# Gates of two more token tiles ahead of the scan phase, and another order of the visits

## The chip, the core and the metric

The kernel runs on one core of a Trainium2 chip. The metric is the time of one execution on the device in microseconds. The median of the runs shown is 2695.26 us (2690.73 to 2696.66 us).

## The reference

The program is one layer of a backbone over 128 context tokens and 2048 latent tokens, 17 tiles of 128 tokens, with a model width of 1024. It computes in this order:

- h = modulated RMSNorm of x, and proj = h @ w_in, cut into q, k, v (3 x 512), a gate (512), 16 columns of scan coefficients, u (512) and vg (512);
- q, k, v through a convolution of width 3 and silu, q and k normalized; then a gated DeltaNet with 4 heads, forward and backward over the tokens, in chunks;
- o_a = rmsnorm(o) * silu(gate) and, per chunk of 128 tokens, o_b = gelu(u) * (ws @ layernorm(gelu(vg)) + bs);
- x = x + ga1 * (concat(o_a, o_b) @ w_out), then a second modulated norm and a squared-ReLU MLP of width 4096, and a final norm.

The recurrence that orders the scan is this step; a chunk needs the state S of the chunk before it:

```
def step(S, xs):
    qd, kd, u_c, w_c, qk_c, gl = xs
    v_new = u_c - einsum('bhck,bhkv->bhcv', w_c, S)
    o = einsum('bhck,bhkv->bhcv', qd, S) + einsum('bhcs,bhsv->bhcv', qk_c, v_new)
    S = S * exp(gl)[..., None, None] + einsum('bhck,bhcv->bhkv', kd, v_new)
```

The outputs are y for the context, y for the latent tokens, and the final states of the context.

## The kernel before, in words

The kernel has three stages. The first projects q, k and v for blocks of three token tiles and stores the normalized rows h to DRAM as a high and a low part (hH_d, hL_d). A product with full precision takes three matmuls: high by high, high by low, low by high (function mm3, lines 217 to 219). In its tail the first stage also loads and splits weights for the next stage, all eight blocks of the gate weights and seven of the eight blocks of the v weights (NV = 7), and the rows of the first HT = 4 token tiles (first_rows).

The second stage is the scan phase, and the change is in it. It has 34 units, one for each token tile and direction: first forward over tiles 0 to 16, then backward. A unit has

- prep_loads (lines 942, 964, 966): a row of decays, the tile's k-by-k products KK and its q-by-k products QK;
- 17 preparation steps: E and its two masked forms (lines 984 to 989), KK scaled and cast to AH, with X (lines 997 to 1004), Y as the transpose of X (lines 1010 and 1012), five levels of two steps each that double a triangular inverse (lines 1028 to 1051), and four closing steps;
- scan_loads, and four scan steps, which carry the state from one unit to the next (lines 959 and 1100 to 1143).

Between these, TensorE gets filler work: for each of the 17 token tiles three groups, g (gate), v and u, of eight steps of three matmuls each (group, one step for each of the eight blocks of 128 input columns). The rows of a tile come by f2_loads (line 1182) into a pool of eight buffers, and a tile needs four. After a group come its finishing steps: for g a tanh, a product and a store (lines 1197 to 1199); for v a gelu (lines 1166 to 1173) and the statistics and centring of 128 tokens (lines 1205 to 1213); for u a gelu and the spatial product (line 1220), which reads the centred vg of its tile, and a store of the result (lines 1224 and 1227). The working buffers of these steps (tags gw, vg and ug) have one buffer each. The groups share four PSUM banks, two of them named pm and two pj, with the spatial products and, later, the output projection. The first four gates use rows and buffers of the pool wp instead.

The order of the work is written out as events with a time. A unit i prepares from i - 2.46 to i - 0.03 and scans from i - 0.51 to i + 1.06 in the forward pass. All filler steps form one list, flat. Its first NF steps are put ahead of everything, at -12 or -8; the rest is spread evenly from -1.61 to 18.16 as fills, and a fill's matmuls are held behind the first matmul of the last preparation or scan step that is emitted before them. The events are emitted in order of time, and a scheduler that simulates the engines then fixes each engine's queue: what is emitted earlier has precedence among what it takes to be ready. On the chip each queue runs in that order. All DMAs are issued by SyncE's queue (SP).

At the start of the phase stand, in order of event time: gates 0 to 3 (-12), the loads of unit 0 (-10), rows of tile 0 (-9), the last block of v weights (-9), the blocks of u weights (-8.5), and then (-8) rows of tile 1, v of tile 0 and one step of u of tile 0. The third stage is the MLP; the change does not touch it.

Of the kernel before, what the change touches and what calls it, by code (L numbers as in the profile page):

```python
# [19 lines left out]
KT = D // P  # L20
DFF = 4096
NT = 17
# [23 lines left out]
NE = 4  # L46
LAG2 = 0
LAG3 = 3
NF = 46
PL = 0  # L50
HT = 4
NV = 7
# [9 lines left out]
def hybrid_step(  # L62
# [137 lines left out]
    def load_w2(gi, k):  # L200
        off = {"g": 1536, "v": 2576, "u": 2064}[gi]
        W2[gi].append(load_split(w_in[0, k * P : (k + 1) * P, off : off + 512]))
# [64 lines left out]
    with ExitStack() as ph:  # L267
# [479 lines left out]
        for bi in range(len(BLOCKS)):  # L747
# [6 lines left out]
            at = {e: n for n, e in enumerate(order)}  # L754
            tile_of = {}
            for n, (gi, h) in enumerate(order):
                u = us[n] if bi == 0 and n < 3 else feature_tile(blk, bi, gi, h)
# [154 lines left out]
    with ExitStack() as ph:  # L912
# [341 lines left out]
        def o_loads(u):  # L1254
            t = u["t"]
            u["of"], u["ga"] = w512("of"), w512("ga")
            load(out=u["of"], in_=of_d[t * P : (t + 1) * P, :])
            load(out=u["ga"], in_=gate_d[t * P : (t + 1) * P, :])
# [74 lines left out]
        def at(time, fn, kind=None):  # L1333
            events.append((time, len(events), fn, kind))

        def spread(t0, t1, steps, kind):
            for j, st in enumerate(steps):
                at(t0 + (t1 - t0) * (j + 0.5) / len(steps), st, kind)

        def scan_step(i, f):  # L1340
            def g():
                u = units[i]
                if "s" not in u:
                    u["s"] = None if i in (0, NT) else units[i - 1]["sn"] if i not in (1, NT + 1) else u["s0"]
                f()
            return g

        def after(i):

            d = 0 if i == 0 else 1  # L1350
            store(out=new_state[0, 0, d].rearrange("h k v -> k h v"), in_=units[i]["sn"])
            s0 = q32("S", 2)
            load(out=s0, in_=state_delta[0, 0, d].rearrange("h k v -> k h v"))
            units[i + 1]["s0"] = s0

        p2, p3 = WINDOWS[:8], WINDOWS[8:]
        for i, u in enumerate(units):
            w = p2 if i <= NT else p3
            at(i - 3 if i > PL else -10, u["prep_loads"])
            at(i - 1, u["scan_loads"])  # L1360
            n = len(u["prep"])
            for j, st in enumerate(u["prep"]):
                at(i - w[0] + (j + 0.5) * (w[0] - w[1]) / n, st, "prep")
            spread(i + w[2], i + w[3], [scan_step(i, f) for f in u["scan"]], "chain")
            if i in (0, NT):
                at(i + w[2] + (w[3] - w[2]) * 0.7, lambda i=i: after(i))
            if i >= NT:
                at(i, lambda u=u: o_loads(u))
                first, second = o_steps(u)
                spread(i + p3[4], i + p3[5], first, "fill")  # L1370
                spread(i + p3[6], i + p3[7], second, "fill")
                if u["t"] > 8:
                    st = h2_steps(u["t"], pj, fraw, w512, fpart, fhalf, lambda u=u: u["x2"])
                    spread(i + p3[8], i + p3[9] + 0.2, st[:5], "fill")
                    spread(i + p3[9] + 0.2, i + p3[9] + 2.1, st[5:], None)
        f2 = [f2_steps(t) for t in range(NT)]
        flat = []
        for n, (t, gi) in enumerate([(t, "g") for t in range(HT)] + [(t, gi) for t in range(HT) for gi in "vu"]
                                    + [(t, gi) for t in range(HT, NT - 2) for gi in "gvu"]
                                    + [(NT - 2, "g"), (NT - 1, "g")]  # L1380
                                    + [(t, gi) for t in (NT - 2, NT - 1) for gi in "vu"]):
            main, later = f2[t][1][gi]
            if gi == "v" and t + 1 < NT - 1 or gi == "g" and t == NT - 2:
                flat.append((KT * n - 0.5, f2[t + 1][0]))
            flat += [(KT * n + j, st) for j, st in enumerate(main)]
            flat += [(KT * n + KT + j + (0.5 if n >= HT else -0.5), st) for j, st in enumerate(later)]
        flat = [st for _, st in sorted(flat, key=lambda e: e[0])]
        at(-9, f2[0][0])
        for j, st in enumerate(flat[:NF]):
            at(-8 if j >= HT * (KT + 1) else -12, st)  # L1390
        for gi in "vu":
            for k in range(NV if gi == "v" else 0, KT):
                at(-9 if gi == "v" else -8.5, lambda gi=gi, k=k: load_w2(gi, k))
        flat = flat[NF:]
        spread(p2[4], p2[5], flat, "fill")
# [412 lines left out]
    for p, (o, n, b) in enumerate(seq):  # L1808
        u = units[n]
# [118 lines left out]
```

## Time and profile before

| | |
|---|---|
| median of the runs | 2695.26 us |
| profiled execution, its own time | 2696.7 us |
| its span, first to last instruction | 2695.0 us |
| TensorE busy | 2628.5 us (98%) |
| VectorE busy | 1866.8 us (69%) |
| ScalarE busy | 1245.5 us (46%) |
| DMA, mean over the span | 216 GB/s |
| granted TensorE clock, mean | 0.993 |

PE is TensorE's matmuls and PEld its weight loads, which overlap them; DVE is VectorE, ACT ScalarE, POOL GpSimd, SP the queue that issues DMAs. In a row of instructions in order of time stand start, duration, engine, line, operation and tiles, and in brackets the idle time before it with what ended that. In a row of a stretch stand the busy times of PE, PEld, DVE, ACT and POOL, the granted clock, the DMA share and the rate. Matmul ends are modelled, and successive matmuls overlap in the rows: their rate is read from their starts.

### The profile page before, as it was taken

What the parts mean: (1) busy time and instruction counts of PE and PEld (TensorE: products, weight loads), DVE (VectorE), ACT (ScalarE), POOL (GpSimd) and SP (SyncE); (2) the same over time, 40 slices, a digit from 0 to 9 for tenths busy, and PEclk for the clock granted to TensorE, in tenths of its full rate; (3) what the DMA queues carried; (4) which work ended last, traced back from release to release, by engine and by line L of the source; (5) the groups of instructions that cost most, each with busy time, mean ns of one, the idle gap of its engine ahead of it and who ended that gap; (6) DMA issues with size and microseconds to landing.
All of it is one profiled execution on the core that took longest, in us unless ns stands there. A gap on an engine that the chain in (4) does not pass through costs nothing.

```text
span 2695.0 us, 45202 instructions
## 1 busy us (share of the span) xinstructions
PE 2628.5 (98%) x15698; PEld 2192.3 (81%) x15698; DVE 1866.8 (69%) x3909; ACT 1245.5 (46%) x3092; POOL 229.5 (9%) x448
## 2 busy tenths in 40 slices
PE   8999999999999899999999999999999999999998
PEld 5999997788887787778887788888888787888887
DVE  5867656877777878885688775665565547774874
ACT  4655555555555656763355543332342432342441
POOL 3111203111111111110000000000000000000000
PEclk9999999999999999999999999999999999999999
DMA  8867539555555657885877797433459979876772
GB/s 297 279 202 224 183 113 299 177 157 161 160 162 157 204 191 232 269 279 181 285 221 228 212 313 228 122 104 106 121 170 371 329 265 309 272 243 215 235 252 94
DMA packets 569388, 580.91 MB, mean 216 GB/s; under 512 B 35693, under 2 KB 401693, under 8 KB 565575
## 3 DMA queue, kind: packets, MB, share of 16 engines
q1 hardware_dynamic: 569158, 578.03, 67.2%
q8 instruction: 123, 2.02, 0.3%
q14 instruction: 107, 0.87, 0.1%
HBM read 398.14 MB, written 179.74 MB: 214 GB/s over the span
## 4 chain that ended last, share of the span: by engine, by line
PE 86%; DVE 6%; DMA 5%; issue 1%; ACT 1%; POOL 0%; SPq 0%; DVEq 0%; POOLq 0%; ACTq 0%
PE f L219 17%; PE f L217 17%; PE f L218 17%; PE pj L217 6%; PE pj L219 6%; PE pj L218 6%; PE pd L959 3%; PE pm L217 1%; PE pm L219 1%; PE pm L218 1%; PE pm L321 1%; PE pt L575 1%; PE pd L1136 1%; PE pd L1137 1%; DMA qT<-qT_d 1%
## 5 line engine op out<-in xcount | busy, mean ns | idle before, releaser
L217 PE MATMUL f<-hop,zH 128*128 128x512 f32 x960 | 376.5, 393 | 1.2 <-ACT zH L1444 1.2
L218 PE MATMUL f<-hop,zH 128*128 128x512 f32 x960 | 377.1, 393 | 0.0
L219 PE MATMUL f<-hop,zL 128*128 128x512 f32 x960 | 376.9, 393 | 0.0
L217 PE MATMUL f<-hop,wH 128*128 128x512 f32 x896 | 354.0, 397 | 0.0
L219 PE MATMUL f<-hop,wL 128*128 128x512 f32 x896 | 351.3, 392 | 0.0
L218 PE MATMUL f<-hop,wH 128*128 128x512 f32 x896 | 351.1, 392 | 0.0
L1444 ACT CAST zH<-zraw 128x512 fp32r<-128x512 f32 x240 | 146.6, 620 | 287.2 <-DVE zraw L1438 86.4
L217 PEld LDWEIGHTS f<-hop,zH 128*128 128x128 f32 x960 | 180.3, 188 | 43.7 <-ACT zH L1444 1.6
L219 PEld LDWEIGHTS f<-hop,zL 128*128 128x128 f32 x960 | 180.3, 188 | 41.9 <-issue 0.9
L218 PEld LDWEIGHTS f<-hop,zH 128*128 128x128 f32 x960 | 180.2, 188 | 41.8 <-issue 0.9
L1438 DVE TENSOR_TENSOR zL<-zraw,zH 128x512 fp32r<-128x512 f32 x240 | 162.9, 686 | 69.1 <-ACT zH L1444 57.7
L219 PEld LDWEIGHTS f<-hop,wL 128*128 128x128 f32 x896 | 168.5, 188 | 37.7
L218 PEld LDWEIGHTS f<-hop,wH 128*128 128x128 f32 x896 | 168.8, 188 | 35.2
L217 PEld LDWEIGHTS f<-hop,wH 128*128 128x128 f32 x896 | 168.8, 188 | 34.7
L217 PE MATMUL pj<-kH,wH 128*128 128x386 f32 (+2 forms) x568 | 190.5, 338 | 0.3 <-DVE kH L473 0.3
L219 PE MATMUL pj<-kH,wL 128*128 128x386 f32 (+2 forms) x568 | 190.3, 335 | 0.0
L218 PE MATMUL pj<-kL,wH 128*128 128x386 f32 (+2 forms) x568 | 189.5, 334 | 0.0
L176 POOL TENSOR_TENSOR r<-rsq,nhalf 128x1 f32<-128x1 f32 (+1 forms) x38 | 23.0, 606 | 1499.3 <-DVE rsq L175 1499.3
L1438 DVE TENSOR_TENSOR wL<-raw,wH 128x512 fp32r<-128x512 f32 x112 | 76.0, 687 | 76.0 <-ACT wH L1444 74.9
L523 DVE SCALAR_TENSOR_TENSOR cv<-pj,vec,cv 128x384 f32<-128x384 f32 (+2 forms) x164 | 87.1, 539 | 58.7 <-ACT cv L520 57.4
L217 PEld LDWEIGHTS pj<-kH,wH 128*128 128x128 f32 x568 | 107.2, 189 | 4.6 <-issue 4.2
L217 PE MATMUL pj<-wH,hH 128*128 128x512 f32 x248 | 109.8, 443 | 0.0
(398 smaller groups left out, 6088.3 us busy)
## 6 DMA issues: line engine op xcount, KB each, us to landing
zraw<-z_d SPq DMA_DIRECT2D x212, 256.0 KB
raw<-in_w_ff_dram SPq DMA_DIRECT2D x128, 256.0 KB
hop<-hop_d SPq DMA_DIRECT2D x28, 1024.0 KB
z_d<-c SPq DMA_DIRECT2D x96, 256.0 KB
zraw<-s_d SPq DMA_DIRECT2D x96, 256.0 KB
raw<-in_w_mod_dram SPq DMA_DIRECT2D x80, 256.0 KB
r<-in_w_ff_dram SPq DMA_DIRECT2D x80, 256.0 KB
s_d<-s SPq DMA_DIRECT2D x64, 256.0 KB
```

The source lines that it names most:

```text
L176: G.tensor_tensor(out=out, in0=t[:np_, :n], in1=nhalf[:np_, :n], op=ALU.pow)
L217: T.matmul(ps, lh, rh, start=first and i == 0, stop=False, skip_group_check=more)
L218: T.matmul(ps, lh, rl, start=False, stop=False, skip_group_check=more)
L219: T.matmul(ps, ll, rh, start=False, stop=last and i == n - 1, skip_group_check=more)
L321: T.matmul(pm[0:2, :], scond[:, k, :], raws[k], start=k == 0, stop=k == KT - 1)
L523: V.scalar_tensor_tensor(out=cv[:, o : o + m], in0=ps[:, s + sh : s + sh + m], scalar=convw[:, w, j : j + 1], in1=cv[:, o : o + m], op0=AL ...
L575: T.matmul(ps[:, i * P : (i + 1) * P], kTt[:, i * P : (i + 1) * P], rhs[:, i * P : (i + 1) * P], start=True, stop=True)
L959: T.matmul(p[:, h, :], lhs[:, h, :], rhs[:, h, :], start=True, stop=True)
L1136: T.matmul(p[:, h, :], u["qT"][:, h, :], s[:, h, :], start=True, stop=False)
L1137: T.matmul(p[:, h, :], u["QK"][:, h, :], u["vn"][:, h, :], start=s is None, stop=True)
L1438: V.tensor_tensor(out=out, in0=a, in1=b, op=op)
L1444: A.copy(h, src)
```

## The change

The front of the filler list becomes longer and its order changes. NF goes from 46 to 62. The list now holds the gates of tiles 0 to 3, then g of tiles 4 and 5, v of 4 and 5, u of 4 and 5, then tiles 6 to 14 with g, v and u each, then v and u of tiles 0 to 3, and tiles 15 and 16 as before. The 62 steps ahead are the four gates (36 steps with their finishing steps) at -12, and g of tile 4, g of tile 5 (each with its finishing step) and v of tile 4 at -8. Rows are loaded for tile 4 at -11.5 and for tile 5 at -9.5; the rows of tile 6 are loaded ahead of u of tile 5, and from then on a tile's rows are loaded ahead of v of the tile visited before it. The loads of unit 0 move from -10 to -12.5, so they are emitted before the first gates.

No computation is added or removed.

```diff
-NF = 46
+NF = 62
...
-            at(i - 3 if i > PL else -10, u["prep_loads"])
+            at(i - 3 if i > PL else -12.5, u["prep_loads"])
...
-        for n, (t, gi) in enumerate([(t, "g") for t in range(HT)] + [(t, gi) for t in range(HT) for gi in "vu"]
-                                    + [(t, gi) for t in range(HT, NT - 2) for gi in "gvu"]
+        visits = [4, 5] + list(range(6, NT - 2)) + list(range(HT)) + [NT - 2, NT - 1]
+        after_visit = dict(zip(visits, visits[1:]))
+        for n, (t, gi) in enumerate([(t, "g") for t in range(HT)] + [(t, gi) for gi in "gvu" for t in (4, 5)]
+                                    + [(t, gi) for t in range(6, NT - 2) for gi in "gvu"]
+                                    + [(t, gi) for t in range(HT) for gi in "vu"]
                                     + [(NT - 2, "g"), (NT - 1, "g")]
                                     + [(t, gi) for t in (NT - 2, NT - 1) for gi in "vu"]):
             main, later = f2[t][1][gi]
-            if gi == "v" and t + 1 < NT - 1 or gi == "g" and t == NT - 2:
-                flat.append((KT * n - 0.5, f2[t + 1][0]))
+            if gi == "v" and t not in (4, 5, NT - 2, NT - 1) or (t, gi) in ((5, "u"), (NT - 2, "g")):
+                flat.append((KT * n - 0.5, f2[after_visit[t]][0]))
...
-        at(-9, f2[0][0])
+        at(-11.5, f2[4][0])
+        at(-9.5, f2[5][0])
         for j, st in enumerate(flat[:NF]):
             at(-8 if j >= HT * (KT + 1) else -12, st)
```

## The prediction, made before the changed kernel had run

> **What bounds the kernel now.** I read the page's engine totals first, then busy time by stretches around the start of the scan phase, then the instructions of that place in order of time on each engine, then the chain of waits. All times are of the profiled execution, which took 2696.7 us (span 2695.0 us and 1.7 us around it); the median of the runs, 2695.26 us, is 1.4 us below it.
>
> ```profile
> span 2695.0 us, 45202 instructions
> PE 2628.5 (98%) x15698; PEld 2192.3 (81%) x15698; DVE 1866.8 (69%) x3909; ACT 1245.5 (46%) x3092; POOL 229.5 (9%) x448
> ```
>
> TensorE is idle for 66 us in all. The next rows (busy time of each engine in a stretch, granted clock, DMA share, GB/s) show where some of that lies.
>
> ```profile
> 440.00:460.00 20.00, 20.00 (x92) 16.51 (x91) 5.98 (x20) 6.86 (x18) 4.19 (x4) 1.00 0.97 290
> 460.00:480.00 20.00, 11.29 (x64) 6.66 (x63) 17.40 (x43) 14.54 (x39) 8.97 (x8) 0.66 0.90 308
> 480.00:500.00 20.00, 18.55 (x148) 13.90 (x147) 17.07 (x44) 8.95 (x23) 2.56 (x3) 1.00 0.67 194
> 515.00:561.00 46.00, 44.32 (x382) 36.47 (x382) 33.35 (x95) 24.76 (x67) 5.62 (x8) 1.00 0.57 167
> 600.00:800.00 200.00, 198.40 (x1687) 164.22 (x1686) 146.10 (x424) 108.89 (x292) 24.13 (x32) 1.00 0.52 159
> ```
>
> So there is a hole at 460 to 480 us: 8.7 us idle, and a granted clock of 0.66. From 515 us the forward scan keeps TensorE full. The hole by instruction:
>
> ```profile
> 455.73 0.39 PE L217 MATMUL pm<-wH,hH 128*128 128x512 f32 x1
> 455.95 0.39 PE L218 MATMUL pm<-wL,hH 128*128 128x512 f32 x1
> 456.18 0.39 PE L219 MATMUL pm<-wH,hL 128*128 128x512 f32 x1
> 456.41 0.39 PE L217 MATMUL pm<-wH,hH 128*128 128x512 f32 x1
> ...
> 462.32 0.40 PE L1010 MATMUL pd<-ident,X 128*128 128x128 f16 x4 [0.59 <-DVE X L1004]
> ...
> 466.70 0.63 PE L219 MATMUL pm<-wH,hL 128*128 128x512 f32 x1
> 470.11 0.37 PE L1032 MATMUL pd<-Y,As 128*128 128x64 f16 x4 [2.77 <-ACT Y L1012]
> ...
> 472.54 0.37 PE L1032 MATMUL pd<-Y,As 128*128 128x64 f16 x4 [0.96 <-ACT Y L1048]
> 472.73 0.77 PE L217 MATMUL pm<-wH,hH 128*128 128x512 f32 x1
> ```
>
> Up to 466.7 us run the 41 front steps (three matmuls each; starts 0.227 us apart at full clock, so a step is 0.68 us). The first fill runs at 472.73 us, behind the sixth preparation step of unit 0 (L1032 of level 4): fills are ordered behind preparation, and the first fill's time -1.61 lies behind six of unit 0's seventeen steps from -2.46 on. What held those steps:
>
> ```profile
> 457.88 1.28 ACT L984 ACTIVATE E<-gb,gcol 128x128 f32<-128x128 f32 x4 [6.79 <-DMA gb<-g_d]
> 459.07 0.60 ACT L1002 CAST AH<-KK 128x512 f16<-128x512 f32 x1
> ...
> 467.79 0.62 ACT L1002 CAST AH<-KK 128x512 f16<-128x512 f32 x1 [3.81 <-POOL KK L999]
> ...
> 469.49 0.56 ACT L1012 CAST Y<-pd 128x512 f16<-128x512 f32 x1
> 463.98 3.77 POOL L999 TENSOR_SCALAR_AFFINE_SELECT KK<-KK 128x512 f32<-128x512 f32 x1 [1.99 <-DMA QK<-qk_d]
> ```
>
> Unit 0's copy Y (L1012) is ready to run from 462.7 us but stands in ScalarE's queue behind unit 1's AH, which waits for a GpSimd select of 3.77 us, itself behind unit 1's loads. That latency is not TensorE work, so it can be covered.
>
> **The change part by part.** *The front (46 to 62 steps of the list).* Before: 4 gate groups, v of tile 0 and one step of u 0, 41 matmul steps. After: the same 4 gates, then g 4, g 5 and v 4: 56. So 15 steps, 45 matmuls, 45 x 0.227 = 10.2 us of TensorE, leave the fills (367 steps become 352) and stand ahead of them.
>
> What that saves later depends on what sets the forward scan's pace. One unit there, from one chain row to the same of the next unit, and its matmuls:
>
> ```profile
> 627.40 1.09 PE pd L959 x8
> 650.13 1.09 PE pd L959 x8
> L217 PE MATMUL pj<-wH,hH 128*128 128x512 f32 x11 | 4.8, 433 | 0.0
> L217 PE MATMUL pm<-wH,hH 128*128 128x512 f32 x8 | 3.7, 459 | 0.0
> L1137 PE MATMUL pd<-vn,QK 128*128 128x128 f32 x8 | 1.5, 275 | 0.0
> L1032 PE MATMUL pd<-Y,As 128*128 128x64 f16 x20 | 1.4, 194 | 0.0
> 508.36 0.89 PE pj L1220 x8
> 485.35 0.28 PE L1045 MATMUL pd<-P,X 128*128 128x64 f16 x4 [0.72 <-DVE P L1036]
> 485.47 0.28 PE L1047 MATMUL pd<-X,P 128*128 128x64 f16 x4
> ```
>
> The period is 22.73 us. By starts and not by overlapping durations: 19 steps x 0.68 = 12.9 us; six groups of eight fp32 128x128 (five like L1137, one L1220) x 0.89 = 5.3 us; three lines of 20 small fp16 (like L1032), each four 0.12 us apart, 1.8 us; some 30 other fp16 matmuls, estimated from the same 0.03 us up to 0.06 us each, 1 to 2 us. That is 21 to 22 of 22.73 us: TensorE sets the pace, and the 10.2 us come off it nearly whole. I take -10.2.
>
> The Trainium skill, "Perfetto Trace Analysis", Identifying the Most-Contended Engine, says that matmul busy time doesn't tell how full TensorE is and that the weight loads' share does. That share is 164.22 of 200 us here, 82%; by it alone a fifth of the period would be free, and the saving could be nothing, as in the third rival.
>
> What it costs in front: v began at 455.73 us without a wait; from there now run 24 steps, 72 x 0.227 = 16.3 us, to 472.1 us. The nearest to a bound below: if unit 0's steps get their turns among them, the first fill comes at about 472.5 us, as now: cost 0. Above: if Y's four matmuls (L1010, earlier 462.32) come only behind the front, what stood from the copy Y to the first fill, 472.73 - 469.49 = 3.2 us, and 0.4 us for Y's matmuls follow 472.1: first fill at 475.7 us, cost 3.0. The front is earlier in emission than the preparation and its inputs are ready, so I take +3.0.
>
> *What feeds the front.* Gates need gate weights only, all built; v 0's last step and u 0 waited for theirs (first row below). The rows of tile 4 take the place of tile 0's, those of tile 5 that of tile 1's:
>
> ```profile
> 461.24 0.49 PE L217 MATMUL pm<-wH,hH 128*128 128x512 f32 x1 [0.59 <-ACT wH L191]
> ...
> 444.24 0.38 SPq L1182 DMA_DIRECT2D hH<-hH_d  x1
> ...
> 449.85 0.90 SPq L1199 DMA_DIRECT2D gate_d<-th  x1
> 450.86 0.36 SPq L964 DMA_DIRECT2D KK<-kk_d  x1
> 451.28 1.10 SPq L1182 DMA_DIRECT2D hL<-hL_d  x2
> 455.60 1.14 DVE L997 SCALAR_TENSOR_TENSOR KK<-KK,beta,Es 128x128 f32<-128x128 f32 x4 [3.16 <-DMA hL<-hL_d]
> ```
>
> The first tile's rows had landed by 455.73 us (v 0 started with no wait); the second's, issued by 452.4 us, are needed at 455.73 + 5.5 = 461.2 us. KK of unit 0, issued at 450.86 us, was used at 455.60 us, 4.7 us later; the same 4.7 us puts tile 5's at 457.1, 4 us early. Cost 0; without that cover, up to 4.7 us once.
>
> *Unit 0's loads from -10 to -12.5.* They were already ahead of the first rows (-9), yet KK was issued behind six row loads, so something other than rank held it, I think the space of its tile. In SP's queue they now pass the stores of the four gates as well, 0.3 to 0.9 us an issue; nothing is queued behind a new wait. I take 0; from 0 to -1.
>
> *Two more gates on ACT and DVE*, in a stretch where DVE is busy 17.40 of 20 us:
>
> ```profile
> 440.05 0.57 ACT L1197 ACTIVATE th<-pm 128x512 f32<-128x512 f32 x1
> 440.65 0.69 DVE L1198 SCALAR_TENSOR_TENSOR th<-th,pm 128x512 f32<-128x512 f32 x1 [0.97 <-ACT th L1197]
> ```
>
> 2 x 0.69 = 1.4 us of DVE, which holds up preparation: +0.7, between 0 and 1.4. Against it, steps at 472.73 us ran at the lower clock, 0.63 to 0.77 us a matmul against 0.39; six of them cost some 1.5 us that a full TensorE would not have paid: -1.5, between -2 and 0 (the new wait of 3 us may lower it again).
>
> The Trainium skill, "TensorE: Matmul & The Clock Gate", What's actually happening, gives about 3.4 us of idleness for the fall and half rate below it. By that rule the new 3.2 us gap would just not lower the clock and the 1.5 us are kept; a gap half a microsecond longer would lose them. The trace's 2.77 us gap behind other short ones did go with 0.66, so the margin is not shown.
>
> *New order of the visits.* Tiles 4 and 5 go g, g, v, v, u, u; tiles 0 to 3 give v and u late, at units 11.6 to 16. In 515 to 561 us fills were v and u alone and DVE was at 33.35 of 46 us, TensorE at 44.32: cost 0 to 1, taken 0. Rows of tile 6 can be issued only as tile 4's u ends, one group ahead of use. The end of the list already has that case:
>
> ```profile
> 860.00 0.91 SPq L1182 DMA_DIRECT2D hL<-hL_d  x2
> 860.00:883.00 23.00, 23.00 (x196) 18.41 (x194) 16.75 (x43) 13.74 (x34) 3.51 (x3) 1.00 0.67 223
> ```
>
> TensorE had no idle time behind it: 0. The sum: -10.2 + 3.0 + 0.7 - 1.5 = -8.0 us, the profiled execution 2688.7, the median 2687.3 us.
>
> **The rivals.** *The hole only moves.* Unit 0's first steps go as a whole behind the front, with all their blocks: from L1010 to the first fill 472.73 - 462.32 = 10.4 us, so first fill at 482.5 us, 9.8 later, and -10.2 + 9.8 = -0.4: 2694.9. For it: in-order queues and the rank of the front. Against it: the blocks (loads of unit 1, the select) ran out at 467.8 us whatever TensorE did.
>
> *Buffers hold DVE (slower).* vg and gw have one buffer. v 5's product into vg must wait until tile 4's spatial matmuls have read it; those now stand behind u 4 and four steps of u 5, 12 steps. A step in the scan takes 22.73 / 17.8 = 1.28 us (352 fills over 19.77 units), so 15.4 us. If that product stands too early in DVE's queue, units 1 and 2 stand behind it. The full price, 15.4, gives -8.0 + 15.4: 2702.7. It decides from 13.4 us of blocking on. For it: queues are fixed ahead and DVE is busy here. Against it: v 0's wait for its own turn would be known to the one who orders the queues, and four PSUM banks let TensorE go on.
>
> *The forward scan does not pay back.* If the recursion and not TensorE sets 22.73 us, the saving is 0 and the front's 3.0 + 0.7 - 1.5 remains: 2697.5. For it: weight loads fill only 164.22 of 200 us. Against it: the starts counted above, 21 to 22 of 22.73 us.
>
> **How the numbers follow.** 0.2% is 5.4 us, about what runs from 2690.73 to 2696.66 can tell from no change. The forecast has 0.56, the hole that moves 0.13, no payback 0.11 (both within 0.2%), the blocked DVE and its like 0.20. The low end takes every term at its best, -10.2 + 0 - 1 + 0 - 2 = -13.2, and some 3 us that I allow for other queue orders: 2679. The high end is the slower rival's, 2702. The forecast's own range is 2682 to 2690.
>
> **What would show it.** Right: g 4 and g 5 directly behind the fourth gate, TensorE busy to about 472 us, idle time at 460 to 480 us down from 8.7 to about 3, first fill at 472 to 476 us, unit periods near 22.1 us, backward scan as before. Wrong: the gap behind 472 us as long as the old one; the period still 22.7 us; DVE waiting at L1173's line for v 5, or matmuls of tile 6 waiting for rows; the start of the backward scan or later stages moved by more than the forward scan's saving.

## The result, and the profile after

The changed kernel is slower: 2701.2 us against 2693.3 us of the kernel before on the same chip, ratio 1.0028, 95% interval 1.0019 to 1.0036, so 7.5 us by the ratio. The profiled execution took 2703.7 us, 7.0 us more than the one before. Single executions of either kernel lie within some 10 us of each other, so places are read from the traces and amounts from the ratios.

The page's totals of the changed kernel:

```profile
span 2702.0 us, 45192 instructions
PE 2629.4 (97%) x15698; PEld 2195.3 (81%) x15698; DVE 1866.3 (69%) x3909; ACT 1247.0 (46%) x3092; POOL 228.7 (8%) x448
```

TensorE does the same work; its idle time rose from 66.5 to 72.6 us. The busy times by stretch (PE, PEld, DVE, ACT, POOL, granted clock, DMA share, GB/s):

```profile
440.00:460.00 20.00, 20.00 (x93) 16.45 (x92) 7.11 (x23) 5.79 (x17) 6.09 (x4) 1.00 0.88 258
460.00:480.00 20.00, 13.88 (x65) 11.23 (x64) 12.73 (x27) 13.84 (x35) 6.59 (x7) 0.95 1.07 362
480.00:500.00 20.00, 17.18 (x130) 12.98 (x130) 16.89 (x47) 10.16 (x26) 3.16 (x4) 0.79 0.48 159
600.00:800.00 200.00, 193.85 (x1670) 160.72 (x1669) 147.31 (x425) 106.98 (x289) 25.53 (x34) 1.00 0.53 160
```

The hole at 460 to 480 us is smaller (6.1 for 8.7 us idle), the stretch behind it is worse (2.8 for 1.5), and the forward scan, which had 1.6 us idle in 200, has 6.2. The front, by TensorE's instructions in order of time:

```profile
457.38 0.39 PE L218 MATMUL pm<-wL,hH 128*128 128x512 f32 x1
...
473.48 0.40 PE L1010 MATMUL pd<-ident,X 128*128 128x128 f16 x4
480.78 0.37 PE L1032 MATMUL pd<-Y,As 128*128 128x64 f16 x4 [6.90 <-ACT Y L1012]
...
483.77 0.37 PE L1032 MATMUL pd<-Y,As 128*128 128x64 f16 x4 [0.52 <-ACT Y L1048]
483.95 0.77 PE L217 MATMUL pj<-wH,hH 128*128 128x512 f32 x1
```

The added steps run without a wait to 473.5 us. Y's matmuls (L1010) come only then, though X, which they read, had been ready since 462.2 us (second fence below). They are followed by 6.9 us of idle time, and the first fill comes at 483.95 us. The execution before had its second gate's tanh at 445.05 us and this one at 446.48; this difference of 1.4 us arose ahead of the added steps and is taken off below ("aligned"). The first fill is then at 482.5 us against 472.73, 9.8 us late. X on VectorE, and what ScalarE did before Y's copy:

```profile
461.80 0.42 DVE L1004 TENSOR_TENSOR X<-ident,As 128x512 f16<-128x512 f16 x1
```

```profile
459.87 0.62 ACT L1002 CAST AH<-KK 128x512 f16<-128x512 f32 x1 [6.57 <-POOL KK L999]
...
468.74 0.62 ACT L1002 CAST AH<-KK 128x512 f16<-128x512 f32 x1 [1.52 <-POOL KK L999]
...
476.38 0.62 ACT L1002 CAST AH<-KK 128x512 f16<-128x512 f32 x1 [3.14 <-POOL KK L999]
476.91 0.61 ACT L191 CAST wH<-raw 128x512 fp32r<-128x512 f32 x1
477.43 1.27 ACT L984 ACTIVATE E<-gb,gcol 128x128 f32<-128x128 f32 x4
...
480.15 0.57 ACT L1012 CAST Y<-pd 128x512 f16<-128x512 f32 x1
```

Unit 0's Y stands in ScalarE's queue behind the AH of unit 1 (468.74) and of unit 2 (476.38), each of which waits for a GpSimd select. Before, one foreign AH stood ahead of it (467.79, in the prediction's last fence of its first part).

How the delay goes on is seen in the copy vn (L1114), one in each unit, here of units 0, 16 and 18, first of the kernel before, then of the changed one:

```profile
505.64 0.59 ACT L1114 COPY vn<-pd 128x512 f32<-128x512 f32 x1 [0.21 <-PE pd L959]
...
873.62 0.59 ACT L1114 COPY vn<-pd 128x512 f32<-128x512 f32 x1 [0.33 <-PE pd L959]
...
925.79 0.59 ACT L1114 COPY vn<-pd 128x512 f32<-128x512 f32 x1 [0.95 <-PE pd L959]
```

```profile
514.66 0.59 ACT L1114 COPY vn<-pd 128x512 f32<-128x512 f32 x1 [2.14 <-PE pd L959]
...
876.65 0.59 ACT L1114 COPY vn<-pd 128x512 f32<-128x512 f32 x1 [0.47 <-PE pd L959]
...
936.06 0.59 ACT L1114 COPY vn<-pd 128x512 f32<-128x512 f32 x1 [1.64 <-PE pd L959]
```

Aligned, unit 0 is 7.6 us late, unit 16 1.6, unit 18 8.8 and the last unit (1277.97 against 1270.93) 5.6. In this execution the forward scan returned 6.0 us (the units' mean period from 0 to 16 is 22.62 us, where it was 23.00) and the turn to the backward scan took 7.2 away. At the turn VectorE waits for a block of output weights (L190) and unit work stands behind it; TensorE then waits 4.37 us and runs at the lower clock. The kernel before has the like wait, but no P directly behind it, and TensorE's longest wait there is 1.4 us. VectorE of the kernel before, then VectorE and TensorE of the changed one:

```profile
883.19 0.49 DVE L190 TENSOR_SCALAR raw<-raw,wscale 128x512 f32<-128x512 f32 x1 [3.10 <-DMA raw<-in_w_out_dram]
883.59 0.68 DVE L1198 SCALAR_TENSOR_TENSOR gw<-gw,pm 128x512 f32<-128x512 f32 x1
```

```profile
884.42 0.49 DVE L190 TENSOR_SCALAR raw<-raw,wscale 128x512 f32<-128x512 f32 x1 [2.77 <-DMA raw<-in_w_out_dram]
884.82 0.69 DVE L192 TENSOR_TENSOR wL<-raw,wH 128x512 fp32r<-128x512 f32 x1
885.43 0.42 DVE L1036 SCALAR_TENSOR_TENSOR P<-pd,identq 128x256 f16<-128x256 f32 x1
```

```profile
885.90 0.37 PE L1045 MATMUL pd<-P,X 128*128 128x64 f16 x4 [4.37 <-DVE P L1036]
...
886.29 0.77 PE L217 MATMUL pj<-wH,hH 128*128 128x512 f32 x1
```

### The profile page after: what moved, and what is told of

Read it like the earlier page. It is cut to its first block, busy times and chain, and to the rows that moved or that the text cites. A ratio compares the mean times of both kernels' runs of the same rounds, so it can differ in the third digit from the quotient of the medians.

```text
span 2702.0 us, 45192 instructions
## 1 busy us (share of the span) xinstructions
PE 2629.4 (97%) x15698; PEld 2195.3 (81%) x15698; DVE 1866.3 (69%) x3909; ACT 1247.0 (46%) x3092; POOL 228.7 (8%) x448
## 4 chain that ended last, share of the span: by engine, by line
PE 83%; DMA 6%; DVE 6%; ACT 2%; issue 2%; SPq 0%; POOL 0%; DVEq 0%; POOLq 0%; ACTq 0%
PE f L219 16%; PE f L217 16%; PE f L218 16%; PE pj L217 6%; PE pj L219 6%; PE pj L218 6%; PE pd L959 2%; DMA qT<-qT_d 2%; PE pm L217 1%; PE pm L218 1%; PE pm L219 1%; PE pd L1136 1%; PE pd L1137 1%; PE pt L575 1%; DMA raw<-in_w_mod_dram 1%
## 5 line engine op out<-in xcount | busy, mean ns | idle before, releaser
L218 PEld LDWEIGHTS pj<-kL,wH 128*128 128x128 f32 x568 | 107.5, 189 | 0.5
```

Source lines behind the costliest of these rows:

```text
L218: T.matmul(ps, lh, rl, start=False, stop=False, skip_group_check=more)
```

## The experiments

Ratios are to the kernel before, each measured beside it, with a 95% interval; 0.001 is 2.7 us.

**Front or order.** The changed kernel with the old length of the front:

```diff
-NF = 62
+NF = 46
```

> The changed kernel with a front of 41 matmul steps as before (NF back to 46: the four gates, g of tile 4, one step of g of tile 5), all else as changed. Theory F, that the longer front puts unit 0's preparation behind it and leaves its latency uncovered: the first fill is back at 473 to 476 us, the start of the scan is lost nothing, the payback in the scan is gone too, and what remains is only the loss at the turn from forward to backward: about +1 to +5 us on before, 2694 to 2698. Theory O, that the new order of visits costs the time: the whole loss stays, 2699 to 2703.

0.9996 (0.9985 to 1.0007). The new order of visits and the earlier loads of unit 0 cost nothing at 41 front steps. The reverse, the kernel before with NF 46 to 62 and nothing else:

> The kernel before with NF = 62 alone: the old order of visits, a front of about as many steps (v 0, u 0 and part of v 1 instead of g 4, g 5, v 4). Theory F: the same lengthened front, Y late, first fill 8 to 11 us later than before, and weights of u waited for in addition: 2697 to 2705. Theory O: without the new order no loss, 2688 to 2694.

1.0020 (1.0010 to 1.0030). This front has 50 matmul steps and not 56, because finishing steps of v and u of tile 0 are among the 62. A longer front is slower in the old order too. So the length is the cause, and not the order.

**The remedies.** Two runs tried to undo the two places that the trace shows. The first emits unit 0's first six preparation steps ahead of g 4, g 5 and v 4:

```diff
-                at(i - w[0] + (j + 0.5) * (w[0] - w[1]) / n, st, "prep")
+                at(-8.2 if i == 0 and j < 6 else i - w[0] + (j + 0.5) * (w[0] - w[1]) / n, st, "prep")
```

> The changed kernel with the first six preparation steps of unit 0 emitted at -8.2, ahead of g 4, g 5 and v 4, so that their matmuls have precedence over the rest of the front. Theory F: Y's matmuls run inside the front, the idle time behind the front falls from 9 us to under 4, the first fill comes 6 to 8 us earlier than in the changed kernel, and the time falls by 5 to 8 us, to 2693 to 2696. Rival: ScalarE's queue holds unit 0 anyway (AH of unit 1 and 2 stand before its copies), the first fill moves by less than 3 us and the time stays at 2699 to 2703.

1.0038 (1.0025 to 1.0050): no gain. Y's matmuls ran at 460.03 us, but Y's copy on ScalarE at 468.96, still behind unit 1's AH, and the next copy (L1048) at 478.63, behind unit 2's. TensorE's order alone was not what held unit 0. The second moves the loads of the output weights away from the turn:

```diff
-WINDOWS = [2.46, 0.03, -0.51, 1.06, -1.61, 18.16, 17.58, 18.3,
+WINDOWS = [2.46, 0.03, -0.51, 1.06, -1.61, 18.16, 17.08, 17.8,
```

> The changed kernel with the loads and splits of the output weights half a unit earlier (17.08 to 17.80 instead of 17.58 to 18.30). If the 5 us lost between units 16 and 18 come from VectorE standing at a weight that has not landed, with the levels of a later unit behind it, these 5 us shrink to 0 to 3: 2695 to 2700. If they come from the new order of the fills, they stay: 2700 to 2703. The front stays as in the changed kernel in both.

1.0014 (1.0003 to 1.0024). Beside 1.0028 some 4 us came back, with intervals that overlap; in the trace unit 16 is 6.4 us late already and unit 18 8.6, so the loss shows earlier instead of going. From unit 16 to unit 18 the five traces with 56 front steps and 352 fills (the changed kernel, these two runs and the last two below) lose 2.2 to 7.2 us against the kernel before, the traces with 41 and 32 front steps lose 0.2 and 4.8, and that of the missing corner below gains 1.6. What sets this is open.

**What a fill is worth in the scan.** The kernel before with fill steps left out and put nowhere, first 15:

```diff
                 def f(k):
+                    if gi == "u" and 1 <= t <= 15 and k == 3:
+                        return
```

> The kernel before, with 15 matmul steps (45 matmuls of 0.227 us, 10.2 us of TensorE at full clock) left out of the fills of the forward scan and put nowhere: the fourth step (k = 3) of group u of tiles 1 to 15, so their outputs lack that part of the sum. The front and everything else stay. This prices the payback alone. Theory T (TensorE sets the scan's pace, my prediction): the whole 10.2 us go, 2686 beside 2696.1 of the kernel before, ratio 0.9962, and the unit period falls from 22.73 to about 22.1 us. Theory R (the recursion and the order of the queues set the pace, my third rival): 0 to 3 us go, 2693 to 2696, ratio 0.999 to 1.000, the period stays and TensorE shows 10 us more idle time.

0.9996 (0.9987 to 1.0005): 45 matmuls or 10.2 us of TensorE less, and 1.1 us less time. In the changed kernel the added front steps were left out in the same way:

```diff
+                    if (t, gi) in ((4, "g"), (5, "g"), (4, "v")) and 2 <= k <= 6:
+                        return
```

> The changed kernel, with the 15 added front steps left out and put nowhere: of g of tile 4, g of tile 5 and v of tile 4 the steps k = 2 to 6 each, so tiles 4 and 5 lack that part of their sums. The front is again 41 steps long, the fills are 352 steps as in the changed kernel. It stands against the changed kernel (ratio 1.0028) by the front alone, and against the version with 41 front steps and 367 fills (0.9996) by the payback alone. Theory T: 10 us less than that version, 2685, ratio 0.996; the front then costs the changed kernel 17 to 18 us, more than its 45 matmuls. Theory R: about the same as that version, 2693 to 2696, ratio 0.999 to 1.000; the front then costs 8 to 10 us, its matmuls and nothing more, and the scan pays nothing back.

1.0002 (0.9993 to 1.0010). Beside 0.9996 of the version with as long a front and 15 fills more, the scan gave nothing back; beside the changed kernel (1.0028) the 15 front steps alone cost 0.0026, 7.0 us. The same stretch of the forward scan in the kernel before, in the kernel before without 15 fill steps, and in the changed kernel without its added front steps:

```profile
500.00:880.00 380.00, 371.86 (x3167) 306.71 (x3164) 282.41 (x814) 205.94 (x548) 51.10 (x65) 1.00 0.53 161
```

```profile
500.00:880.00 380.00, 368.48 (x3136) 304.81 (x3133) 281.29 (x814) 206.00 (x551) 49.03 (x65) 0.98 0.52 159
```

```profile
500.00:880.00 380.00, 363.96 (x3082) 300.21 (x3081) 279.69 (x814) 204.53 (x542) 48.60 (x62) 0.99 0.54 162
```

And the first line of TensorE's waits in that stretch (total, times, longest), in the same order:

```profile
PE pd L1045 <- DVE P L1036: 4.9, 9, 1.6
```

```profile
PE pd L1045 <- DVE P L1036: 7.2, 7, 1.9
```

```profile
PE pd L1045 <- DVE P L1036: 11.6, 12, 3.5
```

Where fills leave, TensorE idles: 8.1, 11.5 and 16.0 us. It waits for P, the step of the triangular inverse that VectorE makes between two of TensorE's. The fills had filled those waits.

Three more doses, with the skipped steps changed to `gi == "v"`, to `gi in "uv"`, and to `gi in "uv" ... k in (3, 4)`:

> The kernel before with another 15 fill steps left out: the fourth step (k = 3) of group v (not u) of tiles 1 to 15, whose outputs lack that part. Same 45 matmuls, 10.2 us. If a fill step is worth about 0.31 us, as 60 of them gave 18.5 us, and the 0.3 us of the first such run was scatter from another order of the queues: 15 x 0.31 = 4.6 us, ratio 0.998 to 0.9985. If the first 15 steps are free because TensorE waits for the chain as soon as fills leave: 0.9990 to 1.0005 again. Whole payback (my prediction): 0.9962.

> The kernel before with both sets of 15 left out, k = 3 of groups u and v of tiles 1 to 15: 30 steps, 20.4 us of TensorE. Even price of 0.31 us a step: 9.2 us, ratio 0.9966. Free at first and dear later (15 for nothing, 60 for 18.5 us, so 0.41 us for each behind the fifteenth): 6.2 us, 0.9977. Whole payback: 0.9924.

> The kernel before with 60 fill steps of the forward scan left out (180 matmuls, 40.9 us of TensorE at full clock): steps k = 3 and 4 of groups v and u of tiles 1 to 15, whose outputs lack those parts. Leaving out 15 of them brought 0.4 us, 0.9996. Theory R in its strict form (the recursion has a period of its own that no fill changes): 0.998 to 1.000, the unit period stays at 22.7 us and TensorE idles some 2.3 us in each. Theory T' (the two are near balance and 15 steps fell into noise): 2660 to 2675, ratio 0.987 to 0.992. Between them, if the chain's own matmuls wait behind fills in TensorE's queue: 0.992 to 0.998, a share of the 40.9 us that is then the price of a fill in the chain.

15 steps of v: 0.9985 (0.9974 to 0.9995). 30 steps: 1.0000 (0.9990 to 1.0009), which none of the three cases had. 60 steps: 0.9929 (0.9912 to 0.9946), 19 of 40.9 us. So by the ratios 15 steps are worth 0 to 4 us and 30 no more, and 60 about half their TensorE time. Single traces scatter more: from unit 0 to unit 16 the forward scan is 0.6 us longer without 15 steps of u, and 8.2, 4.9 and 22.0 us shorter without 15 of v, 30 and 60. Neither theory holds in its strict form; I read this as a scan near balance between TensorE and the chain over VectorE and ScalarE. Which 15 steps leave moves the time by 3 us, which I put down to the order of the queues, but that was not tested.

**What a front step costs.** The same changed kernel with other lengths of the front, NF 36, 54, 27 and 18:

> The changed kernel with NF 62 -> 36: the front holds the four gate groups alone, 32 steps, 24 fewer than the changed kernel and 9 fewer than the version with 41; the fills are 376 steps. Theory T: 9 steps are 27 x 0.227 = 6.1 us of TensorE that go back into the fills, while the front had not set the first fill at 41 steps: 2701, ratio 1.002. Theory R: fills are free, so the time is that of the version with 41 steps or up to 3 us less if the first fill comes earlier: 2692 to 2696, ratio 0.9985 to 1.000.

> The changed kernel with NF 62 -> 54: the front holds the gates of tiles 0 to 5 and one step of v of tile 4, 49 steps, 8 more than the version with 41 and 7 fewer than the changed kernel. If the cost of the front grows with every step (theory R: each step is 0.68 us later for unit 0 and pays nothing back): 0.5 + 8 x 0.55 = 3 to 5 us over the kernel before, ratio 1.001 to 1.002. If the payback is whole and only the hole behind the front costs (theory T), the hole is as deep at 49 as at 56 steps, since the same copies stand behind the same waits: 2696 to 2700. If there is a step between the two, such as the place of unit 0's Y matmuls behind the whole front, the run falls on one side of it: 2695 or 2703.

> The changed kernel with NF 62 -> 27: the front holds three gate groups, 24 steps; the fills are 384 steps. The versions with 32, 41, 49 and 56 front steps stand at 0.9972, 0.9996, 1.0014 and 1.0028, about 0.65 us a step. Theory R (a front step costs its own time, a fill costs nothing): 8 steps less, 5 us less again, 2683, ratio 0.995 to 0.996, as long as the scan has idle TensorE time left. In the version with 32 steps TensorE idles only 4.6 of 300 us at 600 to 900 us, so I expect part of it to be lost: 0.9955 to 0.9975. Theory T (fills cost their time): 2694 or more, ratio 0.999 to 1.001.

> The changed kernel with NF 62 -> 18: two gate groups in front, 16 steps; the fills are 392 steps, 40 (27 us) more than in the changed kernel. Theory R with an end: unit 0's copy Y waits for loads and selects whatever TensorE does, and 392 fills are 25 x 0.68 = 17 us more than the kernel before gives the scan, where it had some 6.5 of 300 us idle; so the gain has run out and turned: 0.997 to 1.001. Theory R without an end: 0.993.

| front steps | fills | ratio (interval) | first fill, aligned, us | foreign AH ahead of unit 0's Y | idle ahead of Y's matmuls, us |
|---|---|---|---|---|---|
| 16 | 392 | 1.0057 (1.0042 to 1.0072) | 465.1 | 0 | 16.48 |
| 24 | 384 | 1.0050 (1.0036 to 1.0064) | 469.1 | 0 | 12.84 |
| 32 | 376 | 0.9972 (0.9963 to 0.9981) | 467.3 | 0 | 3.47 |
| 41 | 367 | 0.9996 (0.9985 to 1.0007) | 473.4 | 1 | 0 |
| 49 | 359 | 1.0014 (1.0002 to 1.0026) | 478.0 | 2 | 0 |
| 56 (the change) | 352 | 1.0028 (1.0019 to 1.0036) | 482.5 | 2 | 0 |

From 32 to 56 steps the first fill goes 15.2 us back for 16.3 us of matmuls, and the time rises by 0.0056, 15 us. If the front steps are paid in full, the 24 fills that left the scan meanwhile gave back about 1 us. Below 32 the first fill moves by about 2 us only: unit 0's X waits for its loads (VectorE's step on KK, L997, for 3.05 us with 24 steps) and TensorE idles. The version with 24 steps:

```profile
461.99 0.61 PE L1010 MATMUL pd<-ident,X 128*128 128x128 f16 x4 [12.84 <-DVE X L1004]
```

From 32 to 24 steps the time rises by 0.0078, 21 us, where the eight fills more are 5.4 us of matmuls. I expected a gain of 5 us or less, and both expectations for 16 steps missed too. TensorE is not short of time there: from 500 to 880 us it is busy for 367.6 us with 24 steps and for 377.4 with 32. In the trace with 24 steps unit 0 is 0.2 us late, unit 4 9.5 and unit 8 13.7; what holds them is open. The version with 32 steps beats both kernels, by 7.5 us and by 15. Its TensorE and ScalarE at the same place:

```profile
463.01 0.61 PE L1010 MATMUL pd<-ident,X 128*128 128x128 f16 x4 [3.47 <-DVE X L1004]
465.59 0.37 PE L1032 MATMUL pd<-Y,As 128*128 128x64 f16 x4 [1.98 <-ACT Y L1012]
...
470.94 0.77 PE L217 MATMUL pm<-wH,hH 128*128 128x512 f32 x1
```

```profile
464.95 0.59 ACT L1012 CAST Y<-pd 128x512 f16<-128x512 f32 x1
...
468.13 0.62 ACT L1002 CAST AH<-KK 128x512 f16<-128x512 f32 x1
```

and its forward scan, with nine fill steps more than before and 2.6 us idle where the kernel before has 8.1:

```profile
500.00:880.00 380.00, 377.38 (x3211) 312.15 (x3210) 286.41 (x832) 208.74 (x557) 49.83 (x65) 1.00 0.55 168
```

**The missing corner.** 56 steps in front and 367 fills, by issuing 15 gate steps of the 41-step version twice:

```diff
                     mm3(u[gi], [(hH[k], hL[k], wh, wl)], first=k == 0, last=k == KT - 1)
+                    if gi == "g" and t < HT and 2 <= k <= (4 if t == 3 else 5):
+                        mm3(u[gi], [(hH[k], hL[k], wh, wl)], first=False, last=False)
```

> The changed kernel with NF 62 -> 46 (41 front steps, 367 fills), and 15 of its gate steps in front issued twice (k = 2 to 5 of g of tiles 0 to 2, k = 2 to 4 of tile 3; these products count double in the gates). TensorE has 56 steps in front as in the changed kernel, and the scan has 367 fills as in the kernel before. It prices the front alone, beside 0.9996 of the version without the doubled steps; the other estimate is the changed kernel against the one with its added steps left out, 1.0028 - 1.0002 = 0.0026, 7 us. Theory R (a front step is paid whole): +7 to +10 us, ratio 1.002 to 1.0035. My prediction's term (the front's cost is 3.0 us, the rest hides in the hole): 1.0007.

1.0045 (1.0032 to 1.0059): 0.0049 or 13 us more than without them, above both estimates, though the interval reaches into theory R's range. The doubled steps lie inside the first four gates, so they delay the gates' finishing steps as well. By the four corners 15 front steps cost 7.0 us (with 352 fills) to 13 us (with 367), and 15 fills less bring between -1.6 us (41 front steps) and 4.6 (56).

**Order and loads with 32 front steps.** The old order (NF 36 in the kernel before), and the 32-step version with the loads of unit 0 back at -10:

> The kernel before with NF 46 -> 36 alone: its own order of visits and unit 0's loads at -10, the four gate groups alone in front. It stands beside the changed kernel with 32 front steps (0.9972) and differs from it by the order and the loads alone. If those cost and bring nothing, as at 41 steps: 0.9965 to 0.998. If they bring something that 41 steps hid: 0.999 or more.

> The version with 32 front steps in the new order (0.9972) with unit 0's loads back from -12.5 to -10. If the gain belongs to the earlier loads, which let unit 0's preparation start under a shorter front: 1.000 to 1.002, like the old order with 32 steps (1.0021). If it belongs to the order of visits: 0.9965 to 0.998.

1.0021 (1.0009 to 1.0034) and 0.9985 (0.9976 to 0.9993). With 32 steps the order brings 0.0036, 9.7 us. That is the second case of each expectation, with 0.9985 just above its 0.998. The loads bring 0.0013 with intervals that overlap. In the old order the trace starts unit 0 earlier and loses it in the scan: unit 4 is 6.4 us early, unit 16 0.9 late. Why is open.

**Whose queue.** Both last runs keep the 56 steps and order unit 1's AH behind unit 0's copies of level 2, and unit 2's AH behind those of level 8, on ScalarE:

```diff
                 A.copy(u["AH"], a)
+                if d == 0 and t in (1, 2):
+                    tc.add_manual_dep(tc.nc.cur_bb.bb.instructions[-1], pin[2 if t == 1 else 8].name, mybir.DependencyInfo(
+                        mybir.DependencyClass.NoSync, mybir.DependencyReason.DATA), reason="order")
...
                     A.copy(x, px)
+                    if t == 0 and d == 0:
+                        pin[s] = tc.nc.cur_bb.bb.instructions[-1]
```

The first also has unit 0's six steps ahead of g 4, g 5 and v 4:

> The changed kernel (56 front steps, 352 fills) with unit 0's first six preparation steps emitted at -8.2, ahead of g 4, g 5 and v 4 (alone: 1.0038), and with unit 1's AH ordered behind unit 0's copies of level 2 and unit 2's AH behind those of level 8 on ScalarE. Theory Q (the place of unit 0's copies in ScalarE's queue makes the front dear): Y's copy runs within 1 us of its matmuls, the first fill comes at 465 to 470 us, unit 0 is no later than before, and the time falls to that of the version with 41 steps or below: 2688 to 2696, ratio 0.997 to 1.000. Theory P (the front steps are paid on TensorE and the scan gives nothing back, whatever ScalarE does): 2702 to 2705, ratio 1.002 to 1.0035.

> The changed kernel with the two orders on ScalarE alone; unit 0's matmuls stay behind the front. Theory Q: Y's matmuls run at 472 us as in the changed kernel, the copy follows at once in place of 6.9 us later, the first fill comes at 476 to 478 us, 5 us earlier than in the changed kernel: 2696 to 2699, ratio 1.0003 to 1.0013. Theory P: unchanged, 2701 to 2703, ratio 1.002 to 1.003.

1.0008 (0.9999 to 1.0017) and 1.0014 (1.0004 to 1.0024). With unit 0's matmuls ahead, the two orders on ScalarE take 0.0030, 8 us, off the 1.0038 that the same step had without them; theory P is out for this run. It did not get to the 41-step version or below, as theory Q wanted, though the intervals meet. The path that theory Q gave is not seen either: the first fill comes at 479.2 us (aligned), not at 465 to 470, and that is only 1.4 us ahead of the run without the two orders; unit 0 is 0.9 us ahead of it. So the ratios say that ScalarE's order is worth 8 us here, and the traces do not show where they are gained. ScalarE in that run:

```profile
465.68 0.56 ACT L1016 CAST Y<-pd 128x512 f16<-128x512 f32 x1
...
473.26 0.62 ACT L191 CAST wH<-raw 128x512 fp32r<-128x512 f32 x1 [3.52 <-DMA raw<-in_w_in_dram]
...
476.77 0.36 ACT L1052 CAST Y<-pd 128x256 f16<-128x256 f32 x1
```

Y came 11 us earlier than in the changed kernel (aligned), but still 6.4 us behind its matmuls; then a weight cast that waits for its load took the place of unit 2's AH, and the second copy came at 476.77 us. In the other run a chain of such casts kept Y's copy 5.7 us behind its matmuls; the first fill came at 480.5 us (aligned), not at 476 to 478, and the gain is within the intervals.

## Why the prediction was wrong

- *Payback, -10.2 us.* This is the step that failed: "TensorE sets the pace, and the 10.2 us come off it nearly whole". Leaving as many out of the kernel before took 1.1 and 4.0 us off it, and twice as many nothing. My count of 21 to 22 us of matmul starts in a 22.73 us period was of a TensorE that fills keep full; it said that TensorE has no room, not that the rest of the unit could go faster. For that the waits for P had to be read: they grow as fills leave. The 6.0 us that the changed kernel's own trace got back by unit 16 are no proof of payback: the version with 56 front steps and all 367 fills got 3.0 us back there, and the turn, which no term of the sum has, took 7.2.
- *Front, +3.0 us.* Mis-sized: the first fill is 9.8 us late, the cost 7.0 us or more. I took "what stood from the copy Y to the first fill", 3.2 us, and so held Y's copy to be immediate. It came 6.7 us after Y's matmuls, behind work of units 1 and 2 on ScalarE, and TensorE idled for 6.90 us.
- *The rivals.* "The hole only moves" gave 482.5 us for the first fill, as measured; "does not pay back" gave the scan's part. I had counted them as alternatives, each with the other's good half. Together, 9.8 - (0 to 4), they give 6 to 10; the ratio gives 7.5. The argument against the first, that the blocks ran out at 467.8 us, took unit 1's AH for the last block; unit 2's came next.
- *Clock, -1.5 us.* Wrong: behind the gap of 6.90 us the matmuls take 0.77 and 0.63 us as before. Nor did the gap of 2.77 us in the kernel before lower the clock: the matmul at 466.70 us, ahead of it, takes 0.63 us already.
- *Nothing for the order of visits, the loads and the rows of tile 6.* Right at 41 steps (0.9996), and TensorE shows no wait for rows. With 32 steps the order is worth 9.7 us, so "nothing" holds only for one length of the front.
- *Two gates on VectorE, +0.7 us.* Not measured apart.
- *Buffers hold DVE.* Not seen: up to the turn VectorE waits at L1173 for a spatial product once, for 0.3 us, and no such wait is among TensorE's in the changed kernel. The turn, where it lost 7.2 us in this trace, was on nobody's list but the last "wrong if".

The Trainium skill, "Perfetto Trace Analysis", Identifying the Most-Contended Engine, judges TensorE by the share of its peak and by its weight loads, not by its matmul busy time. By the 82% of the weight loads there was room, and the removed fills agree: they bought 0 to 4 of 10.2 us. The 60 removed steps, which bought 19 us, don't fit an idle fifth of each period, so the share was the better sign here but not the price.

## What to carry to other kernels

An engine that filler work keeps full is not thereby the bound: leave some filler out and see whether the time falls before pricing a move at its busy time. Work put ahead of a start that waits for loads and copies is paid nearly whole once it reaches past the moment at which that start's inputs are ready, here some 32 steps. In several in-order queues, read for each step of the first unit what stands ahead of it on every engine, since a longer front on one engine reorders the others.

## What the runs showed of the hardware

The granted clock fell behind shorter gaps than I had taken, and the length of one gap does not decide it. In the run with the output weights loaded earlier, a gap of 2.09 us, with no other idle time in the 8 us ahead of it, left the matmuls at half speed. In the changed kernel with its added front steps left out, a gap of 3.50 us left them at full speed for 1.1 us; then they fell to half without another gap:

```profile
858.23 0.33 PE L1045 MATMUL pd<-P,X 128*128 128x64 f16 x4 [2.09 <-DVE P L1036]
...
858.80 0.78 PE L217 MATMUL pj<-wH,hH 128*128 128x512 f32 x1
859.37 0.63 PE L218 MATMUL pj<-wL,hH 128*128 128x512 f32 x1
```

```profile
875.78 0.28 PE L1045 MATMUL pd<-P,X 128*128 128x64 f16 x4 [3.50 <-DVE P L1036]
...
876.32 0.40 PE L218 MATMUL pj<-wL,hH 128*128 128x512 f32 x1
...
876.92 0.37 PE L1047 MATMUL pd<-X,P 128*128 128x64 f16 x4
877.10 0.78 PE L217 MATMUL pj<-wH,hH 128*128 128x512 f32 x1
877.68 0.63 PE L218 MATMUL pj<-wL,hH 128*128 128x512 f32 x1
```

The Trainium skill, "TensorE: Matmul & The Clock Gate", What's actually happening, gives one idle window of about 3.4 us for the fall, in windows that run freely. The gap of 2.09 us is shorter than that; the fall that came 1.1 us after the gap of 3.50 us fits windows that do not begin with the gap.
